# A one-core DeltaNet layer: gate vectors spread by DMA, and the weights' remainders placed later in VectorE's order

## Chip, core and metric

One NeuronCore of a Trainium2 chip runs the whole layer in one launch. The metric is the device time of that launch in microseconds (us). The engines are called as the profile calls them: PE is TensorE (products and transposes), DVE VectorE, ACT ScalarE, POOL GpSimd, SP the sync engine that issues most transfers.

## What is computed

One decoder layer for 256 rows of width 2048, all in float32 (cut to what matters):

```python
mod = silu(c) @ mod_w + mod_b                    # 2048 x 12288
sh1, sc1, ga1, sh2, sc2, ga2 = split(mod, 6)
h = x * (1 + sc1) + sh1
y = gated_deltanet(h, ...)                       # w_in 2048 x 12352, w_out 4096 x 2048
x = layer_norm(2**0.25 * x + (1 + ga1) * y)
h = x * (1 + sc2) + sh2
y = (silu(h @ w_gate) * (h @ w_up)) @ w_down     # 2048 x 11264, 5632 x 2048
x = layer_norm(2**0.25 * x + (1 + ga2) * y)
```

Inside `gated_deltanet` the columns of `h @ w_in` pass a causal convolution over four rows and silu; then, per head and per chunk of the sequence, a unit lower triangular system is solved, and a state is carried from chunk to chunk. The kernel works with two chunks of 128 rows and with four groups q of eight heads.

## The kernel before

**Products in three passes.** Every weight is split into a high part `wh` (rounded to the matmul format, on ACT, L190) and a remainder `wl` (`raw - wh`, on DVE, L191). The activations have two parts as well. `Group.product` issues three products per block of 128 rows: high times high (L223), high times `wl` (L224), low times high (L225). A weight tile is 128 x 1024 (two blocks of k by 512 columns). Twelve products read it: two blocks of k, two halves of the sequence, three passes. Two tiles are a "chunk", and the chunk is the unit of the kernel's own clock `pos[0]`. There are four buffers each for `raw`, `wh` and `wl`, so at most four tiles are alive.

**Order of the work.** The program is written in one pass, but the order on each engine is made by a scheduler: every instruction carries a priority `at(p)`, in chunks, and of the instructions that it takes to be ready the scheduler places the one with the lowest priority. A product of chunk n has priority n to n + 1; the load and the split of its weights have n - 10 (`SPLIT`). Work beside the products is made of tasks (`spawn`, `advance`): each step of a task has as its priority the moment, in chunks, at which it became due. Tasks are the convolutions (six instructions per pair of heads, L470), the decay matrices (L561), the triangular solve of each q (`solve_task`), the state, and the late modulation vectors (`mods_late`). The solve is 62 short dependent instructions on DVE (L584 and L586 in turn) and a transpose, XD (L588), which PE reads at L600. `mods_late` multiplies 128 x 1024 tiles `mraw` of `mod_w` by the condition and adds them up on DVE (L272, first of a sum L271); after 16 of them PE sums over the partitions (L351), ACT copies the sums, PE turns them (L280), and DVE writes the vector (L355). `tp` is the name of the two PSUM buffers that transposes, convolutions and these sums share.

**The gate rows.** `residual` needs 1 + ga1 and 1 + ga2 along the free dimension, the same in all 128 partitions. `gate_row` makes this from the column form (128 x 16) with 16 transposes on PE of a column spread over 128 places (L838) and four copies on ACT (L839). DVE reads the rows at L845, first after the first of the four groups of the output projection, and of the down projection.

In the changed file every line from L191 on stands two lines lower, and those behind `gate_row` three.

Of the kernel before, what the change touches and what calls it, by code (L numbers as in the profile page):

```python
# [8 lines left out]
F32 = mybir.dt.float32  # L9
F32R = mybir.dt.float32r  # L10
I32 = mybir.dt.int32
AF = mybir.ActivationFunctionType
# [4 lines left out]
D = 2048  # L17
S = 256
KT = D // 128
# [10 lines left out]
def gdn_layer_kernel(ctx: ExitStack, tc: tile.TileContext, x, c, mod_w, mod_b, ln_g, ln_b,  # L30
                     w_gu, w_down, w_in, conv_w, a_log, dt_bias, norm_w, w_out, out):
    nc = tc.nc


    SPLIT, MOD0, MODEVERY = 10, 30.0, 0.95
    MGAP, CGAP0, CGAP, CSTEP = 1.5, 1.0, 2.0, 2.3
    CONV, PAIR, SILU = 0.2, 0.4, 2.4
    GDN, LAGAP, LA1, LA2, LA3, SOLVE, HOP = 3.0, 0.5, 0.3, 0.6, 1.5, 5.4, 0.6
# [4 lines left out]
    work = ctx.enter_context(tc.tile_pool(name="work", bufs=2))  # L43
# [3 lines left out]
    dram = ctx.enter_context(tc.tile_pool(name="dram", bufs=2, space=DRAM))  # L47

    act = nc.scalar.activation
# [4 lines left out]
    tr = nc.tensor.transpose  # L54

    @contextmanager
    def at(p):

        old = tc.cur_priority
        tc.cur_priority = int((p + 200) * 1000)  # L60
        yield
        tc.cur_priority = old
# [27 lines left out]
    def tp():  # L90
        return psum.tile([128, 512], F32, name="tp", tag="tp", bufs=2)
# [4 lines left out]
    def f32(t):  # L96
        return t.bitcast(F32)
# [16 lines left out]
    ident = consts.tile([128, 128], F32, name="ident")  # L114
# [18 lines left out]
    p = tp()  # L133
# [16 lines left out]
    p = tp()  # L150
# [31 lines left out]
    def load_split(src, shape, n, lead=None):  # L182

        a, b = shape
        raw = stream.tile([128, a * b], F32, name="raw", tag="raw", bufs=4)
        with at(n - SPLIT if lead is None else lead):
            nc.sync.dma_start(raw.rearrange("p (a b) -> p a b", a=a), src)
            hi = stream.tile([128, a * b], F32R, name="wh", tag="wh", bufs=4)
            lo = stream.tile([128, a * b], F32R, name="wl", tag="wl", bufs=4)
            act(hi, raw, AF.Copy)  # L190
            tt(lo, raw, f32(hi), op=OP.subtract)  # L191
        return hi, lo

    class Group:
# [6 lines left out]
        def chunk(self, k0, lead=None, nk=4, outer=False):  # L201

            if self.ps is None:
                self.ps = [self.alloc(), self.alloc()]
            n = pos[0]
            w = [load_split(wsrc(self.w, k0 + 2 * i, 2, self.c0, 512), (2, 512), n + i / 2, lead)
                 for i in range(nk // 2)]
            order = [(kl, t) for kl in range(nk) for t in range(2)]
            if outer or k0 + nk == self.nk:
                order = [(kl, t) for t in range(2) for kl in range(nk)]  # L210
            for i, (kl, t) in enumerate(order):
                advance(n + i / 8)
                with at(n + i / 8):
                    k = k0 + kl
                    self.product(self.ps[t], k, t, kl, w, k == 0, k == self.nk - 1)
                    if k == self.nk - 1:
                        self.done(t, self.ps[t])
            pos[0] += nk / 4
# [14 lines left out]
    class PartGroup(Group):  # L233
# [6 lines left out]
        def chunk(self, k0, lead=None, nk=4):  # L240
            n = pos[0]
            ps = [self.alloc(), self.alloc()]
            w = [load_split(wsrc(self.w, k0 + 2 * i, 2, self.c0, 512), (2, 512), n + i / 2, lead)
                 for i in range(nk // 2)]
            for t in range(2):
                for kl in range(nk):
                    i = t * nk + kl
                    advance(n + i * nk / 32)
                    with at(n + i * nk / 32):
                        self.product(ps[t], k0 + kl, t, kl, w, kl == 0, kl == nk - 1)  # L250
                with at(n + (t + 1) * nk / 8):
                    if k0 == 0:
                        self.nat = getattr(self, "nat", []) + [self.tiles[t]()]
                        act(self.nat[t], ps[t], AF.Copy)
                    else:
                        tt(self.nat[t], ps[t], self.nat[t], op=OP.add)  # L256
                    if k0 + nk == self.nk:
                        self.done(t, None, self.nat[t])
            pos[0] += nk / 4
# [571 lines left out]
    def gate_row(tag, cols, name):  # L831

        row = held.tile([128, D], F32, name=name, tag=tag)
        for g in range(4):
            p = tp()
            for i in range(4):
                k = 4 * g + i
                tr(p[:, i * 128:(i + 1) * 128], cols[:, k:k + 1].to_broadcast([128, 128]), ident)  # L838
            act(row[:, g * 512:(g + 1) * 512], p, AF.Copy)  # L839
        return row  # L840

    def residual(row, g, t, ps, xin, st):
# [41 lines left out]
    for k0 in range(0, KT, 4):  # L884
# [9 lines left out]
        for i, group in enumerate(first):  # L894
            group.chunk(k0, t0 + CGAP0 + CGAP * i)
    n = pos[0]
    ba_w = [load_split(wsrc(w_in2, 8 * i, 8, 12224, 128), (8, 128), n - 1 + i / 2) for i in range(2)]
    with at(n - 4):
        pp = gd()[:, 0:256]
# [37 lines left out]
    with at(z1 - 2):  # L937
        r = [held.tile([128, D], F32, name=f"r{t}", tag=f"h{t}") for t in range(2)]
        for t in range(2):
            nc.gpsimd.dma_start(r[t], x2[t * 128:(t + 1) * 128, :])  # L940
        row1 = gate_row("h2", ga1, "ga1row")
        st1 = stat_tiles()
# [57 lines left out]
    with at(n0 + 16):  # L1000
        for src, op in ((ln_g, OP.mult), (ln_b, OP.add)):
            row = held.tile([128, D], F32, name="lrow", tag="h2")
# [16 lines left out]
    with tc.tile_pool(name="ph3", bufs=1, reuse_waits="tile") as p3:  # L1019
# [39 lines left out]
        with at(pos[0]):  # L1059
            for key in range(NLATE, 22):  # L1060
                for _ in act_task(key):
                    pass
        row2 = gate_row("h3", ga2, "ga2row")
        r2 = [held.tile([128, D], F32, name=f"rr{t}", tag=f"o{2 + t}") for t in range(2)]
        for t in range(2):
# [32 lines left out]
        for g in range(4):  # L1098
            if g == 1:
                for i, src in enumerate((ln_g, ln_b)):  # L1100
                    for gg in range(4):
                        tag, n = ("sg", 2) if i and gg > 1 else ("an", 6)
# [32 lines left out]
```

## Time and profile before

| | us |
|---|---|
| median of three runs | 1721.46 (1718.86 to 1722.95) |
| the profiled execution | 1717.88 |
| its span, first to last instruction | 1716.1 |
| PE busy in the span | 1661.1 |
| DVE busy | 1138.0 |
| ACT busy | 880.0 |
| POOL busy | 61.5 |

The profiled execution lies 3.6 us below the median, 1.8 us of it outside the span. The mean granted clock of TensorE is 0.996 of full speed. The stages are: 0 to about 220 us the first modulation vectors and the first six column groups; to about 760 the rest of `w_in` with the four solves; to about 955 the output projection; then the norm, gate and up to about 1460, and down to 1700.

### The profile page before, as it was taken

What the parts mean: (1) busy time and instruction counts of PE and PEld (TensorE: products, weight loads), DVE (VectorE), ACT (ScalarE), POOL (GpSimd) and SP (SyncE); (2) the same over time, 40 slices, a digit from 0 to 9 for tenths busy, and PEclk for the clock granted to TensorE, in tenths of its full rate; (3) what the DMA queues carried; (4) which work ended last, traced back from release to release, by engine and by line L of the source; (5) the groups of instructions that cost most, each with busy time, mean ns of one, the idle gap of its engine ahead of it and who ended that gap; (6) DMA issues with size and microseconds to landing.
All of it is one profiled execution on the core that took longest, in us unless ns stands there. A gap on an engine that the chain in (4) does not pass through costs nothing.

```text
span 1716.1 us, 23267 instructions
## 1 busy us (share of the span) xinstructions
PE 1661.1 (97%) x8685; PEld 1324.8 (77%) x8685; DVE 1138.0 (66%) x1635; ACT 880.0 (51%) x1430; POOL 61.5 (4%) x66
## 2 busy tenths in 40 slices
PE   6999999999999999999999999999999999999996
PEld 2666777787887878787787788888878887888885
DVE  2466998958966989847777865764567544455455
ACT  1433669769568667564333744444444444433332
POOL 0000000001001000000000000000000000000003
PEclk9999999999999999999999999999999999999998
DMA  9998785535864777746888586886678666765562
GB/s 346 368 335 289 224 290 189 170 113 160 254 201 122 236 257 242 249 143 234 304 270 288 163 271 192 304 271 186 193 249 287 190 185 214 248 194 192 194 194 99
DMA packets 184082, 390.82 MB, mean 228 GB/s; under 512 B 12112, under 2 KB 14592, under 8 KB 182944
## 3 DMA queue, kind: packets, MB, share of 16 engines
q1 hardware_dynamic: 181952, 378.64, 67.7%
q0 software_dynamic: 2016, 10.68, 1.9%
q8 instruction: 68, 1.11, 0.3%
q14 instruction: 46, 0.38, 0.1%
HBM read 385.08 MB, written 4.19 MB: 227 GB/s over the span
## 4 chain that ended last, share of the span: by engine, by line
PE 73%; DVE 11%; DMA 6%; issue 4%; ACT 4%; POOL 1%; SPq 1%; POOLq 0%; DVEq 0%; ACTq 0%
PE pj L223 20%; PE pj L224 20%; PE pj L225 20%; DMA mraw<-in_mod_w_dram 6%; DVE wl L191 5%; PE gd L224 1%; PE gd L225 1%; ACT wh L190 1%; PE gd L223 1%; DVE macc L272 1%; PE tp L311 1%; DVE X L586 1%; DVE cy L470 1%; DVE tmp L584 1%; DVE LA L561 1%
## 5 line engine op out<-in xcount | busy, mean ns | idle before, releaser
L191 DVE TENSOR_TENSOR wl<-raw,wh 128x1024 fp32r<-128x1024 f32 x522 | 635.2, 1222 | 372.6 <-ACT wh L190 369.5
L190 ACT ACTIVATE wh<-raw 128x1024 fp32r<-128x1024 f32 x522 | 552.3, 1061 | 616.4 <-PE pj L225 472.3
L223 PE MATMUL pj<-wh,h2T 128*128 128x512 f32 x704 | 275.2, 391 | 0.2 <-ACT h2T L972 0.2
L225 PE MATMUL pj<-wh,h2T 128*128 128x512 f32 x704 | 274.5, 390 | 0.5 <-DVE h2T L977 0.5
L224 PE MATMUL pj<-wl,h2T 128*128 128x512 f32 x704 | 273.8, 389 | 0.0
L223 PE MATMUL pj<-wh,hT 128*128 128x512 f32 x640 | 256.5, 403 | 0.0
L224 PE MATMUL pj<-wl,hT 128*128 128x512 f32 x640 | 255.7, 400 | 0.1
L225 PE MATMUL pj<-wh,hT 128*128 128x512 f32 x640 | 255.4, 399 | 0.0
L272 DVE SCALAR_TENSOR_TENSOR macc<-mraw,cond,macc 128x1024 f32<-128x1024 f32 x120 | 153.5, 1279 | 55.8 <-DMA mraw<-in_mod_w_dram 55.3
L225 PEld LDWEIGHTS pj<-wh,h2T 128*128 128x128 f32 x704 | 132.2, 188 | 28.3 <-DVE h2T L977 0.9
L223 PEld LDWEIGHTS pj<-wh,h2T 128*128 128x128 f32 x704 | 132.2, 188 | 27.7 <-ACT h2T L972 0.8
L224 PEld LDWEIGHTS pj<-wl,h2T 128*128 128x128 f32 x704 | 132.2, 188 | 27.0
L223 PEld LDWEIGHTS pj<-wh,hT 128*128 128x128 f32 x640 | 120.5, 189 | 26.5 <-issue 3.3
L224 PEld LDWEIGHTS pj<-wl,hT 128*128 128x128 f32 x640 | 120.6, 188 | 24.7 <-DVE wl L191 0.9
L225 PEld LDWEIGHTS pj<-wh,hT 128*128 128x128 f32 x640 | 120.5, 188 | 23.8 <-issue 0.8
L470 DVE SCALAR_TENSOR_TENSOR cy<-tp,cw,cy 128x255 f32<-128x255 f32 (+2 forms) x192 | 86.1, 475 | 1.3 <-ACT cy L466 1.2
L224 PE MATMUL gd<-wl,hT 128*128 128x512 f32 x128 | 51.7, 406 | 1.4 <-DVE wl L191 1.4
L223 PE MATMUL gd<-wh,hT 128*128 128x512 f32 x128 | 49.9, 398 | 1.9 <-DVE part L256 1.0
L225 PE MATMUL gd<-wh,hT 128*128 128x512 f32 x128 | 51.4, 406 | 0.0
L311 PE MATMUL tp<-mraw,cond 128*32 128x256 f32 x368 | 36.7, 485 | 10.0 <-DMA mraw<-in_mod_w_dram 10.0
L223 PE MATMUL pj<-wh,oTc 128*128 128x512 f32 x112 | 43.9, 392 | 0.0
L225 PE MATMUL pj<-wh,oTc 128*128 128x512 f32 x112 | 43.8, 391 | 0.0
(388 smaller groups left out, 2254.8 us busy)
## 6 DMA issues: line engine op xcount, KB each, us to landing
raw<-in_gdn_w_in_dram SPq DMA_DIRECT2D x194, 512.0 KB, 4.7
mraw<-in_mod_w_dram SPq DMA_DIRECT2D x192, 512.0 KB, 5.4
raw<-in_ffn_w_gu_dram SPq DMA_DIRECT2D x176, 512.0 KB, 4.2
raw<-in_ffn_w_down_dram SPq DMA_DIRECT2D x88, 512.0 KB, 4.7
raw<-in_gdn_w_out_dram SPq DMA_DIRECT2D x64, 512.0 KB, 5.1
x<-in_x_dram SPq DMA_DIRECT2D x8, 256.0 KB, 5.5
r<-in_x_dram POOLq DMA_DIRECT2D x2, 1024.0 KB, 5.0
x1s<-r POOLq DMA_DIRECT2D x2, 1024.0 KB, 6.5
```

The lines of the kernel that those rows point to most:

```text
L190: act(hi, raw, AF.Copy)
L191: tt(lo, raw, f32(hi), op=OP.subtract)
L223: mm(ps, sh, wh, start=start, stop=False)
L224: mm(ps, sh, wl, start=False, stop=False)
L225: mm(ps, sl, wh, start=False, stop=stop)
L272: return stt(acc, w, cond[:, k:k + 1], acc, op0=OP.mult, op1=OP.add)
L311: mm(p[32 * j:32 * j + 32, 0:hw], cond[:, k:k + 1].to_broadcast([128, 32]), raw[:, kl, j * hw:(j + 1) * hw], start=(k == 0), stop=(k == KT ...
L470: stt(y[:, o + s:o + 256], p[:, o:o + 256 - s], tap(3 - s, ct + i), y[:, o + s:o + 256], op0=OP.mult, op1=OP.add)
L561: stt(la[:, s0 + i], src, sc[:, 0, c, h:h + 1], dm[:, i, None, :].to_broadcast([128, 2, 128]), op0=OP.mult, op1=OP.mult)
L584: tt(tv, LD[:, j + 1:32, j:j + 1].to_broadcast([128, n, m]), X[:, j, None, 0:m].to_broadcast([128, n, m]), op=OP.mult)
L586: tt(X[:, j + 1:32, 0:m], X[:, j + 1:32, 0:m], tv, op=OP.subtract)
```

## The change

Two edits. The first takes the remainder (L191, now L193) out of the priority n - 10 and gives it n - 3.5. The transfer and ACT's high part keep n - 10. As a tile can be made about two chunks ahead of its products at the earliest, a ready remainder now stands behind those task steps that became due more than 1.5 chunks ago, and ahead of the younger ones. In the first stage, where `lead` is given, nothing moves.

The second replaces the body of `gate_row`: one transpose of the 128 x 16 columns to 16 x 128, one copy on DVE, a store of 8 KB to DRAM, and a load that reads these 2048 numbers into every partition. Both transfers stand in POOL's queue.

```diff
-    SPLIT, MOD0, MODEVERY = 10, 30.0, 0.95
+    SPLIT, LAG, MOD0, MODEVERY = 10, 3.5, 30.0, 0.95
...
             hi = stream.tile([128, a * b], F32R, name="wh", tag="wh", bufs=4)
             lo = stream.tile([128, a * b], F32R, name="wl", tag="wl", bufs=4)
             act(hi, raw, AF.Copy)
+
+        with at(n - LAG if lead is None else lead):
             tt(lo, raw, f32(hi), op=OP.subtract)
         return hi, lo
...
         row = held.tile([128, D], F32, name=name, tag=tag)
-        for g in range(4):
-            p = tp()
-            for i in range(4):
-                k = 4 * g + i
-                tr(p[:, i * 128:(i + 1) * 128], cols[:, k:k + 1].to_broadcast([128, 128]), ident)
-            act(row[:, g * 512:(g + 1) * 512], p, AF.Copy)
+        p = tp()
+        tr(p[:KT, 0:128], cols, ident)
+        rows = work.tile([KT, 128], F32, name="grow", tag="rows", bufs=2)
+        nc.vector.tensor_copy(rows, p[:KT, 0:128])
+        there = dram.tile([KT, 128], F32, name=f"{name}d", tag=name, bufs=1)
+        nc.gpsimd.dma_start(there, rows)
+        nc.gpsimd.dma_start(row, there.rearrange("k p -> (k p)")[None, :].to_broadcast([128, D]))
         return row
```

**Place 1** is DVE during the solve of the third head group (q = 2), where the second half of the vector ga1 is finished. `cy` is the convolution, `ss` and `rr` belong to the norm of the keys, X and tmp to the solve, macc is the running sum of `mods_late`. Before:

```order
L586 TENSOR_TENSOR X<-X,tmp 128x26x3
L191 TENSOR_TENSOR wl<-raw,wh 128x1024
L584 TENSOR_TENSOR tmp<-LD,X 128x100
L355 SCALAR_TENSOR_TENSOR ga_114<-tp,modb 128x8
L586 TENSOR_TENSOR X<-X,tmp 128x25x4
L191 TENSOR_TENSOR wl<-raw,wh 128x1024
L584 TENSOR_TENSOR tmp<-LD,X 128x96
L271 TENSOR_SCALAR macc<-mraw,cond 128x1024
L586 TENSOR_TENSOR X<-X,tmp 128x24x4
L272 SCALAR_TENSOR_TENSOR macc<-mraw,cond,macc 128x1024
```

and in the changed kernel:

```order
L588 TENSOR_TENSOR X<-X,tmp 128x30
L273 TENSOR_SCALAR macc<-mraw,cond 128x1024
L586 TENSOR_TENSOR tmp<-LD,X 128x58
L357 SCALAR_TENSOR_TENSOR ga_114<-tp,modb 128x8
L588 TENSOR_TENSOR X<-X,tmp 128x29x2
L193 TENSOR_TENSOR wl<-raw,wh 128x1024
L586 TENSOR_TENSOR tmp<-LD,X 128x56
L274 SCALAR_TENSOR_TENSOR macc<-mraw,cond,macc 128x1024
L588 TENSOR_TENSOR X<-X,tmp 128x28x2
L193 TENSOR_TENSOR wl<-raw,wh 128x1024
L586 TENSOR_TENSOR tmp<-LD,X 128x81
L509 TENSOR_SCALAR ss<-ss 128x8
```

With remainders counted from 0 at the start of the program, the one behind the vector's write (L355) was number 144 before, and the one behind L357 is number 136 now; between number 135 and number 136 the changed order has 32 task instructions and no remainder (there were four in the same gap before).

**Place 2** is PE at the same point, around the transposes of the sums (L280, now L282), whose result DVE's write reads. `kq` are keys and queries, `hT` the activations. Before, the four rows of products on either side read the tile of remainder number 140, four ahead of number 144:

```order
L225 MATMUL pj<-wh,hT_118 128x512
L223 MATMUL pj<-wh,hT_116 128x512
L224 MATMUL pj<-wl,hT_116 128x512
L280 MATMUL tp<-ident,sums 128x4 x2
L225 MATMUL pj<-wh,hT_118 128x512
L223 MATMUL pj<-wh,hT_116 128x512
```

and in the changed kernel, where the products around it read remainder number 135 and the next new one is number 136:

```order
L227 MATMUL pj<-wh,hT_119 128x512
L225 MATMUL pj<-wh,hT_117 128x512
L226 MATMUL pj<-wl,hT_117 128x512
L282 MATMUL tp<-ident,sums 128x4 x2
L227 MATMUL pj<-wh,hT_119 128x512
L496 MATMUL tp<-ident,kq 128x128 x4
L225 MATMUL pj<-wh,hT_117 128x512
L226 MATMUL pj<-wl,hT_117 128x512
L496 MATMUL tp<-ident,kq 128x128 x4
```

Seven products and eight transposes now stand between the turned sums and the first product that reads number 136.

**Place 3** is DVE at the end of the first group of the output projection, where `residual` (three instructions per half) begins. Before:

```order
L191 TENSOR_TENSOR wl<-raw,wh 128x1024 x2
L272 SCALAR_TENSOR_TENSOR macc<-mraw,cond,macc 128x1024
L191 TENSOR_TENSOR wl<-raw,wh 128x1024
L845 TENSOR_TENSOR ry<-pj,ga1row 128x512
L846 SCALAR_TENSOR_TENSOR r_7466<-r_7466,ry 128x512
L847 BN_STATS st_7495<-r_7466 128x6
L272 SCALAR_TENSOR_TENSOR macc<-mraw,cond,macc 128x1024
L191 TENSOR_TENSOR wl<-raw,wh 128x1024 x2
```

and in the changed kernel:

```order
L274 SCALAR_TENSOR_TENSOR macc<-mraw,cond,macc 128x1024
L193 TENSOR_TENSOR wl<-raw,wh 128x1024 x2
L274 SCALAR_TENSOR_TENSOR macc<-mraw,cond,macc 128x1024
L848 TENSOR_TENSOR ry<-pj,ga1row 128x512
L849 SCALAR_TENSOR_TENSOR r_7466<-r_7466,ry 128x512
L850 BN_STATS st_7478<-r_7466 128x6
L193 TENSOR_TENSOR wl<-raw,wh 128x1024 x2
```

The multiply-add that stood behind the three residual instructions now stands ahead of them.

## Rows read from the trace of the kernel before

**Rows 1.** The page, busy time of each engine.

```profile
PE 1661.1 (97%) x8685; PEld 1324.8 (77%) x8685; DVE 1138.0 (66%) x1635; ACT 880.0 (51%) x1430; POOL 61.5 (4%) x66
```

**Rows 2.** PE's waits: for whom, us in total, times, longest.

```profile
PE pj L224 <- DVE wl L191: 3.2, 2, 2.5
...
PE gd L600 <- DVE XD L588: 1.9, 4, 1.4
...
PE tp L351 <- DVE tmp L584: 1.5, 1, 1.5
...
PE tp L445 <- DVE q L443: 1.3, 1, 1.3
...
PE gd L556 <- DVE LA L561: 0.8, 1, 0.8
```

**Rows 3.** Busy us of PE, PEld, DVE, ACT, POOL in two stretches.

```profile
550.00:600.00 50.00, 48.50 (x236) 38.78 (x235) 48.23 (x115) 31.83 (x63) 1.64 (x1) 1.00 0.74 232
...
650.00:700.00 50.00, 49.15 (x233) 40.28 (x232) 47.22 (x88) 34.65 (x68) 2.90 (x1) 1.00 0.80 255
```

**Rows 4.** Timeline of PE around the gate transposes: start, duration, instruction.

```profile
789.70 1.03 PE L838 MATMUL tp<-ident,ga 128*128 128x128 f32 x8
790.49 0.48 PE L223 MATMUL pj<-wh,oTb 128*128 128x512 f32 x1
790.81 0.39 PE L224 MATMUL pj<-wl,oTb 128*128 128x512 f32 x1
791.04 0.40 PE L225 MATMUL pj<-wh,oTb 128*128 128x512 f32 x1
791.50 0.65 PE L838 MATMUL tp<-ident,ga 128*128 128x128 f32 x4
791.90 0.48 PE L223 MATMUL pj<-wh,oTb 128*128 128x512 f32 x1
```

**Rows 5.** Timeline of DVE in the solve of q = 2: start, duration, instruction.

```profile
545.84 0.17 DVE L512 TENSOR_SCALAR rr<-rn 128x16 f32<-128x16 f32 x1 [1.37 <-POOL rn L509]
...
596.03 0.23 DVE L584 TENSOR_TENSOR tmp<-LD,X 128x78 f32<-128x78 f32 x1
596.18 0.48 DVE L470 SCALAR_TENSOR_TENSOR cy<-tp,cw,cy 128x255 f32<-128x255 f32 x1
596.57 0.23 DVE L586 TENSOR_TENSOR X<-X,tmp 128x78 f32<-128x78 f32 x1
...
597.90 1.23 DVE L191 TENSOR_TENSOR wl<-raw,wh 128x1024 fp32r<-128x1024 f32 x1
599.05 0.21 DVE L584 TENSOR_TENSOR tmp<-LD,X 128x56 f32<-128x56 f32 x1
```

**Rows 6.** Mean ns of DVE's groups (busy us, mean ns), and L584's min/median/max.

```profile
L191 DVE TENSOR_TENSOR wl<-raw,wh 128x1024 fp32r<-128x1024 f32 x522 | 635.2, 1222 | 372.6 <-ACT wh L190 369.5
...
L272 DVE SCALAR_TENSOR_TENSOR macc<-mraw,cond,macc 128x1024 f32<-128x1024 f32 x120 | 153.5, 1279 | 55.8 <-DMA mraw<-in_mod_w_dram 55.3
...
L584 DVE TENSOR_TENSOR tmp<-LD,X x124: 165/257/303, 305.2 to 720.2; 128x126 f32<-128x126 f32 x12, 128x30 f32<-128x30 f32 x8, 128x56 f32<-128x56 f32 x8, 128x78 f32<-128x78 f32 x8
```

**Rows 7.** Timeline of DVE at the first residual of the output projection.

```profile
818.96 0.69 DVE L847 BATCH_NORM_STATS2 st<-r 128x6 f32<-128x512 f32 x1
820.21 1.28 DVE L272 SCALAR_TENSOR_TENSOR macc<-mraw,cond,macc 128x1024 f32<-128x1024 f32 x1 [0.55 <-DMA mraw<-in_mod_w_dram]
821.41 2.35 DVE L191 TENSOR_TENSOR wl<-raw,wh 128x1024 fp32r<-128x1024 f32 x2
```

**Rows 8.** POOL's transfers (KB, us to landing), and DVE's reads of the rows (first start).

```profile
x1s<-r POOLq DMA_DIRECT2D x2, 1024.0 KB, 6.5
...
lrow<-in_ln_b_dram POOLq DMA_DIRECT2D x1, 1024.0 KB, 7.3
...
L845 DVE TENSOR_TENSOR ry<-pj,ga1row x8: 682/684/692, 817.5 to 956.6; 128x512 f32<-128x512 f32 x8
...
L845 DVE TENSOR_TENSOR ry<-pj,ga2row x8: 677/687/693, 1517.6 to 1701.2; 128x512 f32<-128x512 f32 x8
```

## The prediction

> **What bounds the kernel.** I read the page first: PE is busy 1661 of 1716 us, and no other engine comes near [rows 1]. So a change is worth what it takes from PE's own work or from PE's waits; a shorter queue elsewhere is worth nothing by itself. Next I read PE's waits, and from them those for DVE, since the larger edit rewrites DVE's order [rows 2]: 3.2 us for two remainders `wl`, 1.9 for the solves' XD, 1.5 at L351, 1.3 for q, 0.8 for LA. These are all that a better order on DVE could bring, 8.7 us of 1718. Then I looked at where DVE has room. Its 66% is a mean: in 550 to 600 us it is busy 48.23 of 50 us, in 650 to 700 us 47.22 [rows 3]. These are the stretches of the solves of q = 2 and q = 3, where two engines are full at once. There an order that hands DVE's work to PE in the wrong succession has nothing to catch up with. Last I read the timelines of both engines for durations, above all from start to start, because instructions overlap [rows 4, 5].
>
> **1. The gate rows.** Removed on PE are 32 transposes, 16 per row. The placed ones show their price: eight start at 789.70 and the next product at 790.49, 0.79 us; four take 791.50 to 791.90, 0.40; the product behind a bunch starts after 0.32 instead of 0.23, 0.09 more [rows 4]. With two bunches of eight and four of four that is 2 x 0.79 + 4 x 0.40 + 6 x 0.09 = 3.7 us. Two transposes of 16 rows are added, about 0.15 each (four take 0.40, plus a switch): **-3.4 us**. The eight copies on ACT are off the path, as ACT is half idle [rows 1]. Two copies on DVE of 128 columns cost less than a solve step each, 0.2 us in stretches where the remainders run ahead: nothing.
>
> The new transfers hide or not by when the row is read. The first column vector is complete at about 788 us, just ahead of the old transposes at 789.70 [rows 4]; a store of 1 MB on POOL's queue lands after 6.5 us and a broadcast of 1 MB to all partitions, the same shape as the new load, after 7.3 [rows 8]. The 8 KB store is surely no longer than the 1 MB one. With about 2 us of issues that ends at 804, and L845 first reads at 817.5 [rows 8]: a cover of 13 us. The second vector is finished about 1465 in the trace's order; on a queue with the norm's rows ahead I grant 25 us instead of 14, 1490, against a first read at 1517.6 [rows 8]. Cost 0; if the cover were gone, `residual` and then PE would wait for what lies beyond it.
>
> **2. The solve of q = 2 (places 1 and 2).** Before, remainders were spread through the solve and the PE products that needed them came late: around the turned sums PE worked on remainder 140 of the 144 done. Now the tasks go ahead, and PE turns the sums while it uses number 135, with 136 still to be made. The vector's write waits for the turned sums, so it cannot start before PE gets there, and everything behind it is raced: PE from L282 to the product that reads XD (L602), DVE from L357 to XD. I counted both stretches in the two orders.
>
> DVE: 17 remainders at 1.15 from start to start (19.6), 9 multiply-adds at 1.2 (10.8, the busy mean is 1.28), 24 convolution steps at 0.39 (9.4), 57 solve steps at 0.17 (9.7; 0.15 and more from start to start), 13 other small ones at 0.17 (2.2), the wait of 1.4 for POOL's rn, and XD, an instruction of a remainder's size, 1.1. Together 54.2 us [rows 5, 6]. PE: 199 products at 0.2265 (the distance 790.81 to 791.04 taken over more of them, 45.1), 10 bunches of four transposes at 0.40 + 0.09 (4.9): 50.0 us [rows 4]. DVE is 4.2 us short. If small steps cost 0.15 (1.4 less in 70) and the wait for POOL is covered by ready work (1.4 less), 1.4 us remain: the lower bound; at the mean busy durations (remainder 1.222, multiply-add 1.279, solve step 0.257, convolution 0.48 [rows 5, 6]) DVE would need 63.7 and be 13.7 short, the upper bound. I take the spacing, because these are the distances seen between just such neighbours [rows 5]. Before, q = 2 already waited some 0.2 of the 1.9 (three of the four waits make 0.5 together), so the term is **+4.0 us**. It should show first where a block of 12 convolution steps and 13 solve steps precedes remainder 138.
>
> [...]
>
> The 1.5 us at L351 [rows 2] is really a `tp` buffer not released by the convolution, whose solve steps and remainders stood between. It does not go: L282 takes such a buffer too, and now follows 32 task instructions with convolutions among them. Net 0, bounds -1.5 and +1.5.
>
> **3. The solve of q = 3.** This has the longest XD wait, 1.4 of the 1.9 [rows 2]. By the orders, PE now comes to it 25 products earlier in its work (5.7 us), DVE only two remainders earlier (2.3). Of the 3.4 us between, the 2.8 that DVE idles in 650 to 700 [rows 3] can be filled: **+0.6 us**, bounds 0 and +3.4. For q = 0 and q = 1 the same count leaves DVE in time.
>
> **4. Waits that go.** One multiply-add less (1.2) stands ahead of the norm of q (L443); I count 0.9 of its 1.3. LA (L561) no longer stands behind remainders: -0.8 [rows 2]. Together **-1.7 us**, bounds 0 and -2.1.
>
> **5. The output projection (place 3).** The two waits of 3.2 us [rows 2] come when a multiply-add whose DMA is late (820.21, 0.55 idle) sits between residuals and remainders [rows 7]. Now it stands ahead of the residuals; three instructions of 0.7 [rows 7, 8] stand behind the same transfer, 2.1. The remainder behind is no sooner. **0**, bounds -3.2 and +2.1. From about 1010 us on nothing but the gate copies moves on DVE: 0.
>
> **The sum.** -3.4 + 4.0 + 0.6 - 1.7 + 0 = -0.5. The profiled execution took 1717.9, so 1717.4; the median lies 3.6 above it, so 1721.0 us. About 0.2% (3.4 us) is what a measurement of this kernel can tell from no change.
>
> **The rivals.**
> *Faster: DVE's lead is enough.* PE's waits before are small although DVE is full, so four buffers of remainders may carry the stretch. Then terms 2 and 3 vanish, and if the output projection also profits fully, 3.2 more goes: 1721.0 - 4.6 - 3.2 = 1713.2. For it: the remainders are small in number of waits [rows 2]. Against: the write cannot start before PE turns the sums, so any lead is lost just there.
> *Slower: the shortage comes at every solve.* All four have the same steps, and the same rule moves their remainders back. If q = 1 and q = 3 each lose the 4.2 of q = 2, the time is 1721.0 + 4.2 + 3.6 = 1728.8. It decides as soon as DVE has under 2 us idle in 50 there; q = 3 has 2.8 [rows 3]. [...]
> *Only the gate rows count.* Task and remainder change places without PE noticing: 1721.0 - 4.6 + 1.7 = 1718.1, still within no change.
>
> **How the numbers follow.** Sum as forecast 0.32 and gate rows alone 0.10, both within 0.2%: same 0.42. Faster 0.31. Slower 0.27, 0.03 of it the full durations. Predicted 1721.0. The likeliest case alone spans 1717.5 to 1724.5; the range takes in both other cases with 2 us for their own bounds: 1711 to 1732, leaving out about 1 in 10 on either side.
>
> **What the changed profile would show.** Term 1: no transposes of 128 columns from the gate line, eight copies gone on ACT, and the first L848 with no wait for a row; a wait there of a DMA into the row would refute the cover. Term 2: between 540 and 600 us PE waits for `wl` (now L193) and for XD, 4 us together, and for the vector's write or `tp` at L282; less than 1 us would refute it and make the faster case. Term 3: the last XD wait near 2 us. Term 4: no wait for q or LA. Term 5: two waits for `wl` near 820 and 913 still there. The forecast goes wrong most easily if DVE's spacing in the mixture is not that of the neighbours I took, since 0.05 us on some 120 instructions is 6 us.

## The result, and the profile after

The changed kernel takes 1732.48 us (median of four runs, 1729.60 to 1732.67), the kernel before 1722.20 beside it. The ratio is 1.0065, with a 95% interval of 1.0049 to 1.0080: slower by 8 to 14 us. In a second set of runs it was 1.0054 (1.0037 to 1.0070). The prediction had said 1721.0 with a range up to 1732.0.

The profiled execution has a span of 1730.6 us, 14.5 more than before. First the page, busy time of each engine, to lay beside [rows 1]:

```profile
PE 1666.8 (96%) x8655; PEld 1327.9 (77%) x8655; DVE 1136.8 (66%) x1637; ACT 875.1 (51%) x1422; POOL 62.8 (4%) x70
```

PE has 30 records fewer, as the gate transposes are gone, and yet 5.7 us more of busy time. So part of its work became slower. PE's waits come next (for whom, us in total, times, longest), beside [rows 2]:

```profile
PE tp L531 <- ACT cy L475: 5.4, 3, 2.5
PE pj L226 <- DVE wl L193: 2.9, 5, 1.1
...
PE tp L785 <- DVE oTb L820: 2.7, 1, 2.7
...
PE tp L785 <- DVE oTa L820: 2.2, 1, 2.2
...
PE gd L602 <- DVE XD L590: 2.0, 2, 1.3
...
PE gd L558 <- DVE LA L563: 0.7, 1, 0.7
...
PE tp L447 <- DVE q L445: 0.3, 1, 0.3
```

The waits that the change was argued from have hardly moved, but for q and L351. Three others are new or have grown from almost nothing: L531, which turns the convolved values, and L785, which turns the gated output, once for `oTa` and once for `oTb`. The kernel before has none for `oTa`, and for the other two only this (its lines have lower numbers):

```profile
PE tp L529 <- ACT cy L473: 0.5, 1, 0.5
PE tp L783 <- DVE oTb L818: 0.4, 1, 0.4
```

The stretches of [rows 3], busy us of PE, PEld, DVE, ACT and POOL, then granted clock, DMA share and GB/s, show what else is new:

```profile
550.00:600.00 50.00, 45.78 (x205) 36.84 (x204) 47.31 (x106) 28.50 (x55) 1.64 (x1) 0.93 0.73 242
...
650.00:700.00 50.00, 49.19 (x226) 39.88 (x224) 47.72 (x89) 33.60 (x56) 0.00 (x0) 1.00 0.81 262
700.00:750.00 50.00, 46.48 (x403) 37.92 (x404) 33.47 (x67) 25.21 (x35) 0.00 (x0) 0.97 0.64 202
```

DVE is as full as before and PE idles 4.2 us in the first stretch. Its clock is also no longer whole. The same view in pieces of 5 us finds the place:

```profile
555.00:560.00 5.00, 2.54 (x11) 1.66 (x10) 5.00 (x19) 3.23 (x4) 0.00 (x0) 0.90 0.25 96
560.00:565.00 5.00, 3.25 (x13) 2.71 (x13) 5.00 (x10) 3.05 (x10) 0.00 (x0) 0.50 0.42 113
565.00:570.00 5.00, 5.00 (x24) 4.08 (x23) 4.62 (x7) 2.38 (x5) 0.00 (x0) 0.92 0.95 309
700.00:705.00 5.00, 2.94 (x10) 2.48 (x11) 5.00 (x9) 0.50 (x1) 0.00 (x0) 0.74 0.85 270
970.00:975.00 5.00, 2.14 (x7) 1.75 (x8) 4.97 (x16) 5.00 (x11) 1.15 (x2) 0.70 0.78 284
975.00:980.00 5.00, 5.00 (x20) 3.88 (x18) 4.50 (x8) 3.33 (x7) 0.00 (x0) 0.61 0.38 105
```

From 560 to 565 us the granted clock is 0.50, half of full speed. PE's timeline at the first place (start, duration, instruction, and in brackets the idle time before it and what ended it):

```profile
556.17 0.39 PE L225 MATMUL pj<-wh,hT 128*128 128x512 f32 x1
559.03 1.12 PE L531 MATMUL tp<-ident,cy 128*128 128x128 f32 x4 [2.46 <-ACT cy L475]
561.89 1.12 PE L531 MATMUL tp<-ident,cy 128*128 128x128 f32 x4 [1.75 <-ACT cy L475]
...
564.94 0.63 PE L227 MATMUL pj<-wh,hT 128*128 128x512 f32 x1
565.37 0.61 PE L225 MATMUL pj<-wh,hT 128*128 128x512 f32 x1
```

PE stands still twice, 4.2 us together, and behind it products start every 0.43 us instead of 0.23. DVE at the same time does the block that the prediction pointed at, 12 convolution steps between solve steps, ahead of the next remainder:

```profile
557.08 0.48 DVE L472 SCALAR_TENSOR_TENSOR cy<-tp,cw,cy 128x255 f32<-128x255 f32 x1
557.48 0.25 DVE L588 TENSOR_TENSOR X<-X,tmp 128x96 f32<-128x96 f32 x1
557.64 0.48 DVE L472 SCALAR_TENSOR_TENSOR cy<-tp,cw,cy 128x255 f32<-128x255 f32 x1
...
560.53 1.22 DVE L193 TENSOR_TENSOR wl<-raw,wh 128x1024 fp32r<-128x1024 f32 x1
```

Where the 14.4 us came from can be worked out from the two timelines: each instruction of PE is given the median distance to its successor that its form has in the trace of before, the gate transposes are given none, and the time at which the same sum is reached is compared. Left the time in the kernel before, right what the changed kernel has lost against the row above:

```
   0 to   59   +1.5   first stage, same order (-2.1 to +0.3 against this in other executions)
  59 to  525   +3.5   many small waits (L496, L531, XD of q = 0)
 525 to  604   +8.1   waits at L531, then half clock
 604 to  686   -3.7   0.9 of it waits of before that are gone
 686 to  711   +4.0   wait for oTa, then half clock
 711 to  766   +3.7   wait for oTb, 2.7
 766 to  795   -3.1   the first gate row's transposes, and waits of before that are gone
 795 to  953   -1.2   output projection
 953 to  983   +2.6   half clock behind the first norm's wait
 983 to 1689   -1.0   the second gate row -1.8, small waits +0.8
```

The sum gives every shape one price, wherever it stands. Priced by line and shape, the rows from 525 to 604 and from 604 to 686 become +7.1 and -2.8, and the others stay; so of these two only the total, +4.4, can be relied on. And 14.4 us is more than the 10.3 between the medians: the profiled execution of the kernel before lies 4.3 us under its median of 1722.20, that of the changed kernel at its own. Some 4 us are thus the two executions' own. The +2.6 in the norm is of that kind, as the wait there is the same 2.9 us in both.

### The profile page after: what moved, and what is told of

It is laid out like the page before. It is cut to its first block, busy times and chain, and to the rows that moved or that the text cites. A ratio compares the mean times of both kernels' runs of the same rounds, so it can differ in the third digit from the quotient of the medians.

```text
span 1730.6 us, 23204 instructions
## 1 busy us (share of the span) xinstructions
PE 1666.8 (96%) x8655; PEld 1327.9 (77%) x8655; DVE 1136.8 (66%) x1637; ACT 875.1 (51%) x1422; POOL 62.8 (4%) x70
## 4 chain that ended last, share of the span: by engine, by line
PE 46%; DMA 4%; DVE 3%; issue 2%; POOL 1%; ACT 1%; SPq 0%; POOLq 0%; DVEq 0%; ACTq 0%
PE pj L226 15%; PE pj L227 15%; PE pj L225 15%; DMA mraw<-in_mod_w_dram 4%; DVE wl L193 1%; PE tp L1042 1%; DVE macc L274 0%; POOL rr L1089 0%; ACT wh L190 0%; PE tp L353 0%; PE tp L970 0%; PE tp L785 0%; POOL rr L1090 0%; SPq L187 0%; POOL fo L720 0%
## 5 line engine op out<-in xcount | busy, mean ns | idle before, releaser
L193 DVE TENSOR_TENSOR wl<-raw,wh 128x1024 fp32r<-128x1024 f32 x522 | 634.4, 1222 | 374.9 <-ACT wh L190 368.7
```

## The experiments

Each ratio is to the kernel before on the same chip, with its 95% interval. Most intervals are 0.12 to 0.16% wide to either side, some 2 to 3 us, so the profiles carry the details and the ratios only the large parts.

**The two halves of the change.** `gate_only` sets LAG to 10, `lag_only` restores the body of `gate_row`.

```diff
-    SPLIT, LAG, MOD0, MODEVERY = 10, 3.5, 30.0, 0.95
+    SPLIT, LAG, MOD0, MODEVERY = 10, 10, 30.0, 0.95
```

> Only the gate rows by transfer; the remainders keep their old priority n - 10. Theory A (the loss comes from the new order on VectorE, the gate rows are worth what their transposes cost): 3.4 us less than before, 1718.8 against 1722.2, with 2 us either way for small shifts of order; no wait of TensorE above 2 us at L531 or for oTa/oTb. Theory B (the transfers in POOL's queue, or what stands behind them, bring the loss): 1726 or more.

Measured 0.9973 (0.9962 to 0.9985), 1715.40 against 1720.03: 4.6 us faster. None of the new waits is in its trace (L531 waits 0.5 us, `oTb` 0.3).

> Only the remainders at n - 3.5; the gate rows are made by 32 transposes as before. Theory A: the full loss of the order without the gain of the gate rows, 1732.5 + 3.4 = 1735.9, with the waits at L531 (4.2 us together) still there. Theory B: about 1722, no loss.

Measured 1.0070 (1.0057 to 1.0083): 12 us slower, with the waits for L531 (5.0 us), `oTa` (2.0) and `oTb` (2.7). Theory B falls. The gate rows by themselves are a gain of the expected size, and the remainders' priority is the whole loss. What the gate rows gain beside the moved remainders is not resolved: `lag_only` is only 1 to 3 us above the two sets of runs of the whole change, less than the intervals are wide.

**One stretch back to the old priority.** `undo_q2`, and in the same way `undo_q3` (chunks 80 to 100) and `gate_out` (n - 3.5 from chunk 98 on alone):

```diff
-        with at(n - LAG if lead is None else lead):
+        with at(n - (SPLIT if 64 <= n < 78 else LAG) if lead is None else lead):
```

> The changed kernel with the remainders of chunks 64 to 78 (numbers 128 to 155, the solve of q = 2) back at n - 10, the others at n - 3.5. Theory A: the 8.1 us lost between 525 and 604 us (of before) shrink to about 1, and what is lost near 700 and 775 us stays: about 1725.5. Theory E (the shortage of VectorE is of the whole stretch 540 to 760 us, whatever the order, so that it only moves to the solve of q = 3): 1731 or more.

Measured 1.0023 (1.0014 to 1.0031), where the whole change has 1.0065: 7 us come back with 28 remainders. (In the count of place 1 they are numbers 130 to 157, not 128 to 155, as two remainders of a smaller product come before.) At the same place in the program PE now waits once, 0.8 us, at L531, and its clock stays whole:

```profile
555.00:560.00 5.00, 5.00 (x27) 3.98 (x26) 2.98 (x7) 4.76 (x15) 2.60 (x1) 1.00 0.92 308
560.00:565.00 5.00, 5.00 (x24) 4.14 (x23) 5.00 (x14) 2.13 (x2) 0.00 (x0) 1.00 0.67 216
565.00:570.00 5.00, 4.17 (x21) 3.19 (x20) 4.96 (x13) 2.72 (x6) 0.00 (x0) 1.00 0.76 218
```

Nor does the shortage move to q = 3, as theory E had it: the XD wait there is 1.0 us. The wait for `oTb` stays, 2.6 us, as theory A said. The one for `oTa` does not: it is gone from this trace, and the clock stays whole where it fell near 702 us, although the remainders there still have n - 3.5 (busy times, clock, DMA and GB/s as above):

```profile
700.00:750.00 50.00, 48.86 (x420) 39.39 (x418) 28.93 (x63) 30.36 (x54) 0.00 (x0) 1.00 0.48 146
```

So the 7 us hold the 4.0 us near 700 us too, and not the loss near 560 us alone.

> The changed kernel with the remainders of chunks 80 to 100 (the solve of q = 3) back at n - 10. Theory A: the loss between 695 and 730 us (a wait of 2.4 us for oTa, then products at half clock, 4.0 us together) goes and the 8 us near 560 us stay: about 1728 on the scale of 1722.2 before. Theory H (VectorE is late there only from what was lost at q = 2): the wait for oTa stays, 1732.

Measured 1.0046 (1.0030 to 1.0061); the interval overlaps that of the change, so the gain of some 3 us is not clear of noise in the whole time. In the trace the wait for `oTa` is gone and the clock stays 1.00 in 695 to 705 us, so theory H falls as it was put. But `undo_q2` takes the same wait away. By these two traces it needs both, a DVE that is late from q = 2 and late remainders in q = 3; with either alone it does not come. In the changed kernel DVE and PE stand like this:

```profile
698.43 1.29 DVE L274 SCALAR_TENSOR_TENSOR macc<-mraw,cond,macc 128x1024 f32<-128x1024 f32 x1 [0.17 <-DMA mraw<-in_mod_w_dram]
699.84 1.22 DVE L193 TENSOR_TENSOR wl<-raw,wh 128x1024 fp32r<-128x1024 f32 x1
701.17 0.75 DVE L820 SCALAR_TENSOR_TENSOR oTa<-tp,nwc,oTa 128x512 fp32r<-128x512 f32 x1
```

```profile
702.06 0.81 PE L785 MATMUL tp<-ident,oq 128*128 128x128 f32 x4 [2.21 <-DVE oTa L820]
```

That first split of `oTa` ran at 687.9 us in the kernel before, at 691.8 in `undo_q2`, at 696.9 in `undo_q3`. In the profile of `undo_q3` the stretch from 686 to 711 us costs nothing instead of 4.0; the XD wait of q = 3 grew from 1.3 to 2.1 us, which gave back part of it.

**The wait for `oTb`.** Here DVE itself stands still. Its timeline in the changed kernel, and POOL's instruction that it waits for:

```profile
773.14 0.17 DVE L719 TENSOR_SCALAR ft<-ft 128x16 f32<-128x16 f32 x1
776.37 0.17 DVE L721 TENSOR_TENSOR fo<-fo,rr 128x16 f32<-128x16 f32 x1 [3.06 <-POOL fo L720]
776.58 1.14 DVE L797 SCALAR_TENSOR_TENSOR oq<-oq,fo,nat 128x128 f32<-128x128 f32 x4
777.64 1.40 DVE L820 SCALAR_TENSOR_TENSOR oTb<-tp,nwc,oTb 128x512 fp32r<-128x512 f32 x2
```

```profile
773.40 2.93 POOL L720 TENSOR_TENSOR fo<-ft,mhalf 128x16 f32<-128x16 f32 x1 [14.05 <-DVE ft L719]
```

Before, the wait for POOL at this place was 0.6 us, because a remainder and a split (2.0 us) stood between:

```profile
764.83 2.93 POOL L718 TENSOR_TENSOR fo<-ft,mhalf 128x16 f32<-128x16 f32 x1 [0.58 <-DVE ft L717]
```

```profile
765.31 1.23 DVE L191 TENSOR_TENSOR wl<-raw,wh 128x1024 fp32r<-128x1024 f32 x1 [0.56 <-ACT wh L190]
766.45 0.75 DVE L818 SCALAR_TENSOR_TENSOR oTb<-tp,nwc,oTb 128x512 fp32r<-128x512 f32 x1
767.80 0.18 DVE L719 TENSOR_TENSOR fo<-fo,rr 128x16 f32<-128x16 f32 x1 [0.60 <-POOL fo L718]
```

Now nothing does, and the splits that would free PE's `tp` buffers are queued behind L721.

```diff
-        nc.gpsimd.tensor_tensor(f..., t..., mhalf, op=OP.pow)
+        (nc.vector if q == NQ - 1 else nc.gpsimd).tensor_tensor(f..., t..., mhalf, op=OP.mult if q == NQ - 1 else OP.pow)
```

> The changed kernel, but for the last head group the power on GpSimd (L720, 2.93 us) is replaced by a product on VectorE of about 0.2 us; that group's output norm is left out by it. The order of the other instructions near it is almost the same. Theory F (VectorE stands 3.06 us at L721 for GpSimd, with the two splits L820 behind it that TensorE's transposes wait for): the wait of 2.7 us for oTb near 775 us goes, 2.7 us gained, about 1729.5 on the scale of 1722.2 before; a further 1 to 2 us if the granted clock no longer falls behind it. Theory G (TensorE would wait there for other work in any case): 1732.

Measured 1.0034 (1.0020 to 1.0049), about 5 us less than the change (3 less than its second set), and no wait for `oTb`; in its profile the stretch from 740 to 766 us costs 2.8 us less than in the changed kernel. Theory F holds for the wait; the size of the gain is only known to some 4 us. (Its profile, with 2.8 us of wait at XD, is of an execution of 1733.81 us, 7 above the median.)

**The half clock.** `fill_l531` keeps PE busy ahead of the two bunches, without touching DVE's order there:

```diff
-        p = tp()
+        p = tp(); [tr(p[:, 0:128], ident, ident) for i in range({0: 20, 2: 14}[h] if (q, half) == (3, 0) else 0)]
```

> The changed kernel, with 34 unneeded transposes (20 and 14) on TensorE ahead of the two bunches of L531 that waited 2.5 and 1.8 us near 560 us; they overwrite nothing that is read and take 3.4 us of the 4.2 in which the engine stood still, so that it doesn't idle there. Both theories: the granted clock stays at 1.00 from 555 to 570 us, and products there start every 0.23 us instead of 0.43. Theory C (the half clock is a loss of its own, on top of the wait): about 3 us gained, 1729.5. Theory D (VectorE's stretch to XD sets the end; the half clock only used up time that TensorE would have waited for XD, which it now finds ready 0.7 us early): 0.7 us gained or nothing, 1732, and a new wait for XD of about 2 us at 603 us.

Measured 1.0045 (1.0033 to 1.0058), 1726.61 us. The clock stays whole with the same two bunches still behind the convolution; PE idles 0.6 us ahead of each filling, 1.2 instead of 4.2:

```profile
555.00:560.00 5.00, 4.39 (x33) 3.76 (x31) 5.00 (x19) 3.24 (x4) 0.00 (x0) 1.00 0.29 104
560.00:565.00 5.00, 4.39 (x33) 3.83 (x32) 5.00 (x11) 3.54 (x11) 0.00 (x0) 1.00 0.33 99
565.00:570.00 5.00, 5.00 (x26) 4.15 (x25) 5.00 (x7) 2.23 (x4) 0.00 (x0) 1.00 0.90 292
```

From L282 to the first product that reads XD, PE takes 58.05 us in the changed kernel (546.59 to 604.64) and 55.74 here (546.89 to 602.63). So the filling was worth 2.3 us in this stretch. By an estimate from these rows the half clock had cost some 3, as the filling takes 3.8 us (557.44 to 559.65 and 560.85 to 562.41) and replaces 3.0 of idleness. Theory D's new wait of 2 us did not come, since DVE's XD was ready 1.6 us sooner too (602.42 instead of 603.98): DVE had been waiting on the slowed PE in its turn. The longest of these waits, 0.9 us for a high part at 574.18, is behind a step of ACT that itself had waited 1.7 us for PE. The total had gained more than these 2.3, so the pair was repeated on one chip:

> The changed kernel once more, unaltered, to stand beside the next one on the same chip: 1.0065 of before, between 1.005 and 1.008, in every theory.

> The kernel of the first filling (34 unneeded transposes ahead of L531), on the same chip as the changed kernel. Theory C (the half clock is a loss of its own): 0.9975 to 0.9985 of the changed kernel, 2.5 to 4 us, with 1.00 granted from 555 to 570 us. Theory D (only VectorE sets the end of that stretch): 0.9995 or more of the changed kernel.

Measured 1.0054 (1.0037 to 1.0070) and 1.0042 (1.0027 to 1.0058). Their quotient, 0.9988, lies between what theories C and D had said. The medians, 1730.42 and 1727.31, are 3 us apart, but the intervals overlap. The stretch is again shorter, 56.4 us against 58.0. That adding 34 unneeded transposes shortens it by 1.6 to 2.3 us is shown by the profiles; what it is worth in the whole time lies between about 0 and 5 us.

> The gate rows by transfer, remainders at n - 10, and 26 unneeded transposes on TensorE (2.6 us) ahead of the bunch of L970 that waits 2.9 us for VectorE in the first norm, in an order that stays nearly the same otherwise. Theory C: the granted clock stays 1.00 there, where it fell to 0.72 in 960 to 965 us with the gate rows alone; up to 0.75 us gained, 0.996 to 0.998 of before. Theory K (the clock falls there for another reason than TensorE's idleness): the granted clock falls all the same, no gain.

```diff
-        p = tp()
+        d = gd(); [tr(d[:, 0:128], r[t][:, (k + i % 4) * 128:(k + i % 4 + 1) * 128], ident) for i in range(26 if (t, k) == (0, 12) else 0)]; p = tp()
```

This failed as an experiment. The filling stands ahead of products on which the norm itself depends, so DVE was late by as much, the wait of 2.9 us stayed, and behind it the clock fell to 0.78 in 965 to 970 us. Measured 0.9985 (0.9970 to 1.0000). It decides nothing between C and K.

**Other values.**

> The changed kernel with n - 7 in the place of n - 3.5: of the tasks only those that have waited for over 5 chunks go ahead of a ready remainder. Theory A (the loss comes with the blocks of tasks ahead of a remainder): nearer to the gate rows alone than to the changed kernel, 0.998 to 1.001 of before. Theory J (any shift away from n - 10 breaks an order that was fitted to it): 1.004 or more.

Measured 1.0022 (1.0007 to 1.0037): between 1.0065 at 3.5 and 0.9973 at 10, somewhat more than theory A allowed and less than theory J's 1.004. In its profile L531 waits 2.1 us in place of 5.4, but LA waits 2.4 and `oTb` 2.6.

> The gate rows by transfer, and n - 3.5 only from chunk 98 on (the output projection), where no solve runs. Theory A: no loss, as no task is due in a block there; the waits for remainders, 4.5 us with the gate rows alone, fall by 1 to 3 us: 0.9960 of before, between 0.994 and 0.998. Theory I (also there the later remainder brings waits): 1.000 or more.

Measured 0.9983 (0.9968 to 0.9997), no better than the gate rows alone. The waits for remainders are 3.5 us instead of 4.5, but the two traces of the changed kernel differ by more (2.9 and 1.2). Whether the later remainder helps or hurts there stays open; the lowest ratio of all is that of `gate_only`, and the intervals of the two overlap.

## Why the prediction was wrong

**Gate rows: right.** -3.4 us were forecast and 4.6 measured, with 2.6 to 6.5 in the interval. The transfers hide as argued: the store is issued at 798.40 and lands 3.3 us later, the load is issued at 801.94 and lands 9.3 us later, and L848 first reads the row at 834.2. The 2 us granted for the two issues were the author's estimate; they took 0.51 and 0.55 us.

**The solve of q = 2: the count was right, the price too small.** DVE's stretch from L357 to the end of XD was counted at 54.2 us from start-to-start distances. It measures 53.9 and 54.7 in the two runs with filling, where PE keeps its clock, and 55.8 in the changed kernel. The durations of the same instructions add up to 62.6 us in the first of the two, 8.7 more than the stretch took: its length goes by the spacing, not by the durations. The upper bound of 63.7 was a slip, as the durations named there make 63.2.

PE takes 58.05 us where the count had 50.0. Its own work is 50.8 (in `fill_l531`: 55.74 less 1.2 of waits and 3.8 of filling); it idles 4.2 at L531; and the half clock adds some 3. Two things were left out. DVE starts behind PE, not level with it: L357 runs at 548.19, 1.6 us after L282 at 546.59. With the count of PE's work 0.8 too low this makes a shortage of 5.0 us in `fill_l531` (3.8 filled, 1.2 idle), so that 4.2 us of idleness in the changed kernel equal the 4.2 of the count only by chance. And PE's idleness has its own price, the half clock, for which the sum has no term. The wait also shows at a reader that the prediction didn't name: of the two things that DVE was late with, XD and the convolution, PE comes to the convolution first. That 525 to 686 us cost +4.4 in all, near the +4.0 of the term, is errors that cancel: the 1.5 us at L351, which were to stay, are gone, and 0.9 us of waits behind the solve.

**The solve of q = 3: the step that failed.** The term of +0.6 looked at XD alone, and put what else DVE hands to PE in that stretch at nothing. The XD wait did stay as it was (1.4 before, 1.3 after; 0.4 to 3.0 in the other traces with the remainders at n - 3.5 throughout). But 686 to 766 us lose 4.0 and 3.7. The same full stretch delivers the splits of the gated output: `oTa` waited behind remainders and multiply-adds, 2.2 us and then 0.74 of the clock. And behind it L721 put POOL's 2.9 us in DVE's way. By the runs that undo them the two are worth about 3 and 5 us, with some 3 to 4 us of uncertainty each; that the waits go is shown by the traces.

**Waits that go.** q went from 1.3 to 0.3, as said. LA went from 0.8 to 0.7 in this trace and to 0.5 in the second one of the changed kernel; in `lag_only` and with filling it is gone. And 59 to 525 us, costed at nothing beside these, lost 3.5 in small waits. The 8.7 us that the prediction began with were not all of PE's waits for DVE either: the 0.4 us for `oTb` stood in the same list, and the 0.5 for `cy` stood there under ACT, behind which are DVE's convolution steps. Two of the three handovers that came to cost most were to be seen there as small waits.

**Output projection: right in size.** 2.9 us of waits for remainders instead of 3.2, and 1.2 in the second trace; at the two places that were named, 1.1 and 0.7 us instead of 0.7 and 2.5.

So the slower rival, "the shortage comes at every solve", had the right side at 0.27, though not the mechanism: not XD at each solve, but whichever result of DVE PE reads first behind a block, and the clock after it. The nearest of all, 1730.7 with the term of q = 2 at full durations (its upper bound of 13.7 in the place of 4.0), is near by luck, as the stretch that it lengthens took 53.9 to 55.8 us. The gains of the single undoings, q = 2 (7), q = 3 (3) and `fo` (5), can't be added up to the loss, since the first two both hold the wait for `oTa`. What is shown is that the order of the remainders makes the whole loss, and that putting back 28 of them, in the solve of q = 2, takes some 7 us off.

## What to carry to other kernels

Where two engines are both full, a new order on one of them must be checked against every instruction of the other that reads from it, and not only against the reader that waits now: list what is handed over in the stretch and when it comes, the small waits of now among it. A rule that lets old tasks go first moves everything that was spread out into blocks; what stands in a block is late as a whole. An instruction that waits for a slow helper (here 2.9 us on POOL) is covered by what happens to be queued ahead of it, so a reordering that takes that away uncovers it.

## What the hardware showed

A wait of PE costs more than its length when the clock falls behind it: products 0.43 us apart instead of 0.23, for 3 to 7 us (in the changed kernel 559 to 566, 702 to 706 and 972 to 979 us). It is not the wait's length alone that decides. The wait of 2.9 us in the first norm is the same in every run; in the kernel before the granted clock stayed whole behind it, as these rows show, and in the changed kernel it went to 0.61 (above).

```profile
955.00:960.00 5.00, 2.21 (x13) 1.28 (x11) 3.60 (x11) 5.00 (x12) 0.78 (x2) 1.00 0.68 206
960.00:965.00 5.00, 4.61 (x24) 3.44 (x24) 5.00 (x14) 5.00 (x10) 0.38 (x1) 1.00 0.52 184
```

Of the thirteen traces the clock fell behind this wait in eleven; `undo_q2` is the other in which it stayed whole. The wait of 2.1 us for `oTa` left it whole in `fill_again`, and in the second trace of the changed kernel, where it is as long, the granted clock is 0.71 from 700 to 705 us. The 2.7 us for `oTb` left it whole in the first trace of the changed kernel.

Waits of the same length thus end either way, and no run here shows what decides it. For the sum this means that a wait of some 2 us can have two prices, and that the executions of one kernel differ by some of them.
